# A two-layer hybrid decoder on one core: norm sums of the first layer from a token-major copy of x, early MLP items of four row tiles, and another issue order of the odd norm

## The chip, the cores and the metric

The kernel runs on one core of one Trainium2 chip. The metric is device time in microseconds of one execution, the median of three runs. Five engines work beside each other, each through its own in-order queue: PE (TensorE, matrix products), DVE (VectorE), ACT (ScalarE), POOL (GpSimd) and SP (SyncE, which here issues all DMAs of weights and inputs).

## What is computed

The reference is a decoder trunk of two layers over 1024 tokens of 1024 features in float32. Cut to what matters here:

```
def rmsnorm(x, g):
    y = x * lax.rsqrt(jnp.mean(x * x, axis=-1, keepdims=True) + NORM_EPS)
    return y * g

for layer in range(2):
    hn = rmsnorm(h, mix_norm[layer])
    if layer % 2 == 0:
        h = h + sparse_pool_mixer(hn, ...)   # indexer, top 256 keys a query, attention; causal pooling; one output projection
    else:
        h = h + gated_deltanet(hn, ...)      # projection, short convolution, chunked delta rule
    h = h + squared_relu_mlp(rmsnorm(h, mlp_norm[layer]), w_ff1[layer], w_ff2[layer])
return rmsnorm(h, final_norm)

squared_relu_mlp = lambda h, w1, w2: jnp.square(jax.nn.relu(h @ w1)) @ w2     # 1024 -> 4096 -> 1024
```

## The kernel before

**Layout and products.** The tokens are worked in two halves of 512. Features lie on partitions, so x is eight tiles of 128 x 512 a half, and a norm's sum over features goes over partitions. Every product of float32 operands is made of three matmuls (`mm3`, L244 to L246): high by high, high by low and low by high part. A weight chunk of 128 x 512 comes by DMA from SP (L199), ScalarE copies its high part (L164), GpSimd takes the rest (L168, `rest`); a buffer ring holds four raw chunks. SP issues the loads in the order of the program, with eight semaphores in turn.

**Norms.** `add_square` squares a tile on ScalarE (L304) and adds it to a sum on VectorE (L307). `rstd_cols` sums over partitions with small matmuls against ones (L287), and `rsqrt` makes the reciprocal root on VectorE (L263 to L268). `over_partitions` (L275) spreads it by four transposes, and `normed` scales the tiles. The first half of the even norm is written out in `even_first` (squares, adds at L416), beside the first two projections, which take x with its gain but not yet its scale; `even_second` does the second half through `squares`.

**The even layer.** First projections, scores of the indexer, and the search for the top 256 keys of each query on VectorE and ScalarE (L630 to L698; the last part, L694 to L698, picks the keys of one block of queries). Attention of the second half (`attend`, L710 to L774) comes after the search. Beside the later search and the attention a generator `fill` puts out the MLP of the first half in items: `f1` products (`project`), their squared ReLU (`squared`, L809 to L811 and L168), and `f2` products, which `accumulate` adds into the residual h (L825). In `mlp_order` an item group is two row tiles of the hidden 4096, so each of eight tiles of h gets six matmuls and one VectorE add a group. `even_out` is the output projection of a half, from the attention's tiles and the pool mixer's tiles `yb`; for the second half it runs when `fill` has reached a set point. What is left of the first half's MLP runs in `alone`.

**The odd layer.** `odd_heads` begins with the odd norm of the first half beside the second half's MLP: `norm_stages` gives out squares, then the root, then the normed tiles, each at a `next(norm)`, between items of `fill`:

```
for n in (3, 2, 2):
    for _ in range(n):
        next(fill)
    next(norm, None)
```

A list scheduler orders each engine's instructions from this program order, priorities (`high_priority`, `ahead_by`) and `queued()`, which ties a step to the last matmul issued.

Of the kernel before, what the change touches and what calls it, by code (L numbers as in the profile page):

```python
# [18 lines left out]
OP = mybir.AluOpType  # L19
# [15 lines left out]
FILL = (5.6, 4.7)  # L35
BANKS = {"even": {"g": 2, "o": 1, "s": 1, "t": 4}, "odd": {"g": 2, "o": 1, "d": 2, "t": 3}}
# [87 lines left out]
class Trunk:  # L124
# [257 lines left out]
    def even_scales(self, acc):  # L382

        r = self.rstd_cols(acc, D, self.small(4, "even_r"))
        n8 = self.small(4, "even_n8")
        self.nc.vector.tensor_scalar(n8, r, -0.125, None, op0=OP.mult)
        r8 = self.small(4, "even_r8")
        self.nc.vector.tensor_scalar(r8, r, 0.125, None, op0=OP.mult)
        self.scales.append((r, n8, r8))

    def even_first(self):
# [9 lines left out]
        acc = self.T.get()  # L401
        for k in range(KT):
# [22 lines left out]
        self.even_scales(acc)  # L425
# [389 lines left out]
    def accumulate(self, key, st, a, s, chunks=range(4)):  # L815

        nc = self.nc
        for c in chunks:
            w = [t.rearrange("p (n c) -> p n c", n=2) for t in self.chunk((key, c), st)]
            for m in (2 * c, 2 * c + 1):  # L820
                ps, cs = self.bank("t" if self.solo and m % 2 else "d"), slice(m % 2 * P, (m % 2 + 1) * P)
                for n in range(2):
                    self.mm3(ps, w[0][:, n, cs], w[1][:, n, cs], a[n][:, 0:512], a[n][:, 512:1024], n == 0, n == 1)
                h = self.h[s][m]
                nc.vector.tensor_tensor(h, ps, h, op=OP.add)  # L825
                yield T_ROWS

    def mlp_order(self):

        for g in range(FF // 256 + 1):  # L830
            for n in range(2):
                yield (g if g < FF // 256 else None), n, g - 1, (2 * n, 2 * n + 1)

    def mlp_half(self, l, s, x, ring):

        a = {}
        for g, n, before, chunks in self.mlp_order():  # L840
            if g is not None:
                ps = self.project(("f1", l, 2 * g + n), x, st="m")
                if n == 0:
                    a[g] = [self.squared(ps, ring)]
                self.pending = n == 1
                yield T_COLS
            if before >= 0:
                yield from self.accumulate(("f2", l, before), "m", a[before], s, chunks)
            if g is not None and n == 1:
                a[g].append(self.squared(ps, ring))  # L850
                self.pending = False

    def mlp_units(self, l):
        out = []
        for g, n, before, chunks in self.mlp_order():
            if g is not None:
                out += [((("f1", l, 2 * g + n), c), self.I["w1"][l, 2 * g + n][:, c * 512:(c + 1) * 512], 512)
                        for c in range(2)]
            if before >= 0:
                out += [((("f2", l, before), c), self.I["w2"][l, before, c], 512) for c in chunks]  # L860
# [245 lines left out]
    def odd_heads(self, fills):  # L1106
# [107 lines left out]
    def even(self):  # L1214
# [3 lines left out]
        with ExitStack() as st:  # L1218
# [12 lines left out]
            with ExitStack() as st3:  # L1231
# [9 lines left out]
                for n, _ in enumerate(self.even_steps(0, x, EVEN_A, first)):  # L1241
                    if n == 7:
# [41 lines left out]
            fill = self.mlp_half(0, 0, self.x0, self.Y)  # L1284
            take(fill, 12)
            while self.background:
                take(fill, 2)
                self.tick(1)
            st2.close()
            with ExitStack() as st2:  # L1290
# [3 lines left out]
                for _ in range(8):  # L1294
# [11 lines left out]
        return fill  # L1306
# [58 lines left out]
    def run(self):  # L1365
        a, b = self.odd_units()
        m = [self.mlp_units(l) for l in range(2)]
        self.plan(a=self.even_units() + a, o=b, m=m[0] + m[0] + m[1] + m[1])
        self.h = [[None] * KT, [None] * KT]
        with ExitStack() as st:  # L1370
            self.banks("even", st)
            fill = self.even()
# [3 lines left out]
        self.alone(fill, "below", 3 * len(m[0]))  # L1376
        below = lambda: self.mlp_half(0, 1, x, self.Y)

        def above():
# [3 lines left out]
            yield from self.mlp_half(1, 0, xa, self.Y)  # L1383
# [8 lines left out]
        self.alone(self.mlp_half(1, 1, x, self.Y), "above", 0)  # L1392
# [3 lines left out]
def layouts(x, mix_norm, mlp_norm, w_ff1, w_ff2, ev_w_in, ev_kv_norm, ev_w_uk, ev_w_uv, ev_pool_w, ev_pool_scale,  # L1396
# [11 lines left out]
    def pairs(w):  # L1408

        return c(w.reshape(-1, 2, P, 4, 256).transpose(0, 3, 2, 1, 4).reshape(-1, 4, P, 512))  # L1410

    cols = lambda v: np.asarray(v).reshape(-1, P).T
# [7 lines left out]
        "xt": c(x[0].T), **const_tables(), "prm": c(prm), "rope": rope_table(),  # L1420
# [4 lines left out]
        "woo": pairs(od_w_out[0]), "w1": np.stack([tiles(w) for w in w_ff1]), "w2": np.stack([pairs(w) for w in w_ff2]),  # L1425
    }
# [21 lines left out]
```

## Time and profile before

| | us |
|---|---|
| three runs | 2812.59, 2803.46, 2809.56 |
| median | 2809.56 |
| profiled execution, its own time | 2807.27 |
| its span, first to last instruction | 2805.5 |
| TensorE busy | 2652.1 (95%) |
| VectorE busy | 1702.2 (61%) |
| GpSimd busy | 1229.8 (44%) |
| ScalarE busy | 1185.3 (42%) |

The profile is of one execution, in us from its first instruction. TensorE's matmuls are pipelined: a row's duration is longer than the distance to the next. The granted clock is the share of TensorE's full speed that the chip let it have. "Idle before" an instruction is put down to what released it last.

### The profile page before, as it was taken

Reading aid. Unit: us, or ns where it says so; the run is one execution under the profiler, and the core shown is the slowest. Engines: PE = TensorE matmul, PEld = TensorE weight load, DVE = VectorE, ACT = ScalarE, POOL = GpSimd, SP = SyncE. Lnnn points to the kernel's source line nnn. Section 1 sums busy time; section 2 is a strip of 40 time slices with the busy share of each in tenths; the row PEclk is TensorE's granted clock in tenths of the full one; section 3 lists DMA queues with packets and bytes.
Section 4 is the critical chain, followed back from the end, with each engine's and each line's share of the span. In section 5 each row is a group of like instructions: output and inputs, shape, how many; then the busy total and the mean of one; then the engine's idle time right before and its main releaser. Section 6 shows DMA issues by size and latency. Waiting matters only on the chain. (4 is left out here: it accounts for less than half of the span.)

```text
span 2805.5 us, 44654 instructions
## 1 busy us (share of the span) xinstructions
PE 2652.1 (95%) x16648; PEld 2093.2 (75%) x16648; DVE 1702.2 (61%) x3649; ACT 1185.3 (42%) x2472; POOL 1229.8 (44%) x1062
## 2 busy tenths in 40 slices
PE   8788979999999899999999999999999999899998
PEld 6566758787787677777777767777777777688886
DVE  6898899735535555655565677665555645633334
ACT  5657767234533443433333444433343323433332
POOL 5642364442235444444444434444443434544442
PEclk9999989999999999999999999999999999999999
DMA  5221233231123222222222211122222222333332
GB/s 174 65 75 31 66 97 96 85 94 57 39 65 97 68 80 72 83 69 72 74 77 76 72 43 61 60 70 71 70 83 76 65 65 87 120 97 96 98 97 77
DMA packets 119916, 218.81 MB, mean 78 GB/s; under 512 B 13970, under 2 KB 15122, under 8 KB 119698
## 3 DMA queue, kind: packets, MB, share of 16 engines
q1 hardware_dynamic: 119698, 215.95, 25.1%
q8 instruction: 131, 2.15, 0.3%
q14 instruction: 87, 0.71, 0.1%
HBM read 207.51 MB, written 4.19 MB: 75 GB/s over the span
## 5 line engine op out<-in xcount | busy, mean ns | idle before, releaser
L168 POOL TENSOR_TENSOR wm<-raw,wm 128x512 fp32r<-128x512 f32 x420 | 555.4, 1323 | 843.4 <-ACT wm L164 825.2
L164 ACT ACTIVATE wm<-raw 128x512 fp32r<-128x512 f32 x420 | 264.1, 629 | 612.1 <-PE ps_g L245 306.5
L168 POOL TENSOR_TENSOR w<-raw,w 128x512 fp32r<-128x512 f32 x222 | 297.1, 1339 | 374.3 <-ACT w L164 348.5
L825 DVE TENSOR_TENSOR h<-ps_d,h 128x512 f32<-128x512 f32 x396 | 269.9, 685 | 139.3 <-PE ps_d L246 136.6
L811 DVE SCALAR_TENSOR_TENSOR ps_g<-ps_g,temps 128x512 f32<-128x512 f32 x128 | 89.2, 696 | 308.0 <-ACT temps L809 308.0
L244 PE MATMUL ps_g<-x,w 128*128 128x512 f32 (+1 forms) x644 | 257.6, 400 | 12.0 <-ACT w L164 8.9
L245 PE MATMUL ps_g<-x,w 128*128 128x512 f32 x644 | 256.0, 398 | 3.3 <-DVE x L379 2.5
L244 PE MATMUL ps_d<-y,wm 128*128 128x512 f32 x600 | 246.8, 412 | 11.8 <-DVE h L825 8.0
L246 PE MATMUL ps_g<-x,w 128*128 128x512 f32 (+1 forms) x644 | 255.5, 397 | 1.0 <-POOL w L168 1.0
L164 ACT ACTIVATE w<-raw 128x512 fp32r<-128x512 f32 x222 | 139.0, 627 | 275.5 <-PE ps_g L245 190.1
L245 PE MATMUL ps_d<-y,wm 128*128 128x512 f32 x600 | 238.8, 398 | 0.0
L246 PE MATMUL ps_d<-y,wm 128*128 128x512 f32 x600 | 238.4, 397 | 0.1
L246 PE MATMUL ps_g<-xb,wm 128*128 128x512 f32 x512 | 205.0, 400 | 15.6 <-POOL wm L168 15.6
L244 PE MATMUL ps_g<-xb,wm 128*128 128x512 f32 x512 | 205.6, 401 | 3.9 <-ACT qkvz L930 2.3
L932 DVE SCALAR_TENSOR_TENSOR qkvz<-temps,conv,qkvz 128x512 f32<-128x512 f32 x144 | 133.9, 930 | 122.3 <-ACT qkvz L930 121.1
L245 PE MATMUL ps_g<-xb,wm 128*128 128x512 f32 x512 | 204.3, 399 | 0.0
L244 PEld LDWEIGHTS ps_g<-x,w 128*128 128x128 f32 (+1 forms) x644 | 122.0, 190 | 41.1 <-ACT w L164 9.6
L244 PE MATMUL ps_g<-x,wm 128*128 128x512 f32 x348 | 141.3, 406 | 9.3 <-ACT wm L164 5.2
L246 PE MATMUL ps_g<-x,wm 128*128 128x512 f32 x348 | 140.3, 403 | 10.0 <-POOL wm L168 10.0
L825 DVE TENSOR_TENSOR h<-ps_t,h 128x512 f32<-128x512 f32 x180 | 123.2, 687 | 43.6 <-PE ps_t L246 43.3
L245 PEld LDWEIGHTS ps_g<-x,w 128*128 128x128 f32 x644 | 121.6, 189 | 32.9 <-DVE x L379 4.6
L244 PEld LDWEIGHTS ps_d<-y,wm 128*128 128x128 f32 x600 | 112.7, 188 | 44.0 <-DVE h L825 14.2
(430 smaller groups left out, 6159.1 us busy)
## 6 DMA issues: line engine op xcount, KB each, us to landing
raw<-in_w_dram SPq DMA_DIRECT2D x512, 256.0 KB, 2.6
raw<-in_woi_dram SPq DMA_DIRECT2D x128, 256.0 KB, 2.6
raw<-in_wei_dram SPq DMA_DIRECT2D x52, 256.0 KB, 2.7
raw<-in_weo_dram SPq DMA_DIRECT2D x32, 256.0 KB, 2.6
raw<-in_woo_dram SPq DMA_DIRECT2D x32, 256.0 KB, 2.7
h<-in_xt_dram SPq DMA_DIRECT2D x16, 256.0 KB, 3.5
at<-at SPq DMA_DIRECT2D x64, 64.0 KB, 2.0
out_dram<-temps SPq DMA_DIRECT2D x16, 256.0 KB, 2.1
```

Source lines behind the costliest of these rows:

```text
L164: self.nc.scalar.activation(out, in_, AF.Copy)
L168: eng.tensor_tensor(lo, full, hi.bitcast(F32), op=OP.subtract)
L244: mm(ps, wh, xh, start=start, stop=False)
L245: mm(ps, wh, xl, start=False, stop=False)
L246: mm(ps, wl, xh, start=False, stop=stop)
L811: nc.vector.scalar_tensor_tensor(ps, ps, 0.0, r, op0=OP.max, op1=OP.mult)
L825: nc.vector.tensor_tensor(h, ps, h, op=OP.add)
L932: nc.vector.scalar_tensor_tensor(acc, pin[:, j:j + 512], cw(j), acc, op0=OP.mult, op1=OP.add)
```

## The change

**Sums of the even norm.** A second copy of x, `xr`, with tokens on partitions, comes in as 16 more loads of 128 x 512 (256 KB each). `even_sums` squares each in place on ScalarE and sums along the row in the same instruction (`accum_out`); `even_scales` adds the two half sums and takes the root. The adds at L416, the small matmuls for these two norms and the squares and adds of `even_second` are gone. The second half's sums are issued beside the first projections.

**Items of four.** 28 of the 32 row tiles of the first half's MLP (`EARLY` = 7 groups) go in groups of four, with a second arrangement of the `f2` weights (`w2q`): a tile of h gets twelve matmuls in one PSUM bank and one add a group, so 56 adds fewer in all. The squared tiles take the rings `Y` and `PB` in turn. The items are paced by their estimated time (`beside`), all 28 tiles are issued ahead of `even_out` of the second half, and the splits of its `yb` tiles (a ScalarE copy and a GpSimd rest each, four tiles) go to the attention's own ring `pb`, so they can only come when attention is done with it. Before, they were at 349.98 to 358 us. The last four row tiles stay in groups of two, in `alone`.

**The odd norm.** The first `next(norm)` comes ahead of the first items.

```diff
+    def even_sums(self, s, cs):
+        nc = self.nc
+        for c in cs:
+            for n in range(2):
+                t = self.H[1].get()
+                at = s * HL + c * P
+                nc.sync.dma_start(t, self.I["xr"][at:at + P, n * 512:(n + 1) * 512])
+                nc.scalar.activation(t, t, AF.Square, accum_out=self.sums[s][:, 4 * n + c:4 * n + c + 1])
-    def even_scales(self, acc):
-        r = self.rstd_cols(acc, D, self.small(4, "even_r"))
+    def even_scales(self, s):
+        t, m = self.sums[s], self.small(4, "rs_m")
+        self.nc.vector.tensor_tensor(m, t[:, 0:4], t[:, 4:8], op=OP.add)
+        self.nc.vector.tensor_scalar(m, m, 1.0 / D, EPS, op0=OP.mult, op1=OP.add)
+        r = self.rsqrt(m, 4, self.small(4, "even_r"))
...
             self.gained(h, k, x)
-            sq = self.T.get() if k else acc
-            nc.scalar.activation(sq, h[k], AF.Square)
-            if k:
-                nc.vector.tensor_tensor(acc, acc, sq, op=OP.add)
+            if k >= 4:
+                self.even_sums(0, (k - 4,))
...
-        self.even_scales(self.squares(hs))
...
-            for m in (2 * c, 2 * c + 1):
-                ps, cs = self.bank("t" if self.solo and m % 2 else "d"), slice(m % 2 * P, (m % 2 + 1) * P)
-                for n in range(2):
-                    self.mm3(ps, w[0][:, n, cs], w[1][:, n, cs], a[n][:, 0:512], a[n][:, 512:1024], n == 0, n == 1)
-                h = self.h[s][m]
+            for m in range(4 // n):
+                ps, cs = self.bank("t" if self.solo and m else "d"), slice(m * P, (m + 1) * P)
+                for k in range(n):
+                    self.mm3(ps, w[0][:, k, cs], w[1][:, k, cs], a[k][:, 0:512], a[k][:, 512:1024], k == 0, k == n - 1)
+                h = self.h[s][4 // n * c + m]
                 nc.vector.tensor_tensor(h, ps, h, op=OP.add)
...
-        for n in (3, 2, 2):
+        for n in (4, 2, 2):
+            next(norm, None)
             for _ in range(n):
                 next(fill)
-            next(norm, None)
...
                 for n, _ in enumerate(self.even_steps(0, x, EVEN_A, first)):
+                    if n < 2:
+                        self.even_sums(1, (2 * n, 2 * n + 1))
+                    if n == 2:
+                        self.even_scales(1)
...
-            fill = self.mlp_half(0, 0, self.x0, self.Y)
-            take(fill, 12)
+            fill, due = self.mlp_half(0, 0, self.x0, (self.Y, self.PB), 0, EARLY, 4), 0.0
+            def beside(us):
+                nonlocal due
+                due += us
+                while due > 0:
+                    if len(self.queue["m"]) < self.after_early + 8:
+                        self.room("m", self.WM)
+                    due -= next(fill, 1e9)
+            beside(27.0)
             while self.background:
-                take(fill, 2)
+                beside(4.5)
                 self.tick(1)
...
-                    take(fill, 2)
+                    beside(4.5)
                 for _ in att:
-                    take(fill, 1)
-            self.room("m", self.WM)
-            while self.pending or any(t[3] is not self.WM for t in self.ready["m"]):
-                next(fill)
-            for _ in self.even_out(1, ya, self.yb[1], self.PB):
-                pass
+                    beside(3.0)
+                beside(1e6)
+                for _ in self.even_out(1, ya, self.yb[1], pb):
+                    pass
```

How the order of instructions moves, at three places. Lines of the changed kernel are shifted: L288 is the old L287, L276 the old L275, L308 the old L307, L836 the old L825, L822 the old L811, L169 the old L168, L704 to L709 the old L693 to L698, and L244 to L246 are now L245 to L247.

PE at the odd norm of the first half (`ps_d`: the last `f2` products of the fill; L287: sums over partitions; L275: the root spread; `x,w`: odd projections of the first half; `xb`: fill of the second half), before:

```order
3058 L245 MATMUL ps_d<-y,wm 128x512
3059 L246 MATMUL ps_d<-y,wm 128x512
3060 L287 MATMUL ps_t<-ca,temps 128x2 x4
3061 L275 MATMUL ps_t<-ca,rs_y 128x128 x4
3062 L244 MATMUL ps_g<-x,w 128x512
3063 L244 MATMUL ps_g<-xb,wm 128x512
```

and now, with 16 more rows of the same `ps_d` products where the dots are:

```order
3043 L247 MATMUL ps_d<-y,wm 128x512
3044 L288 MATMUL ps_t<-ca,temps 128x2 x4
3045 L245 MATMUL ps_d<-y,wm 128x512
...
3062 L247 MATMUL ps_d<-y,wm 128x512
3063 L276 MATMUL ps_t<-ca,rs_y 128x128 x4
3064 L245 MATMUL ps_g<-xb,wm 128x512
3065 L246 MATMUL ps_g<-xb,wm 128x512
```

The sums and the spreading, neighbours before, now have 18 full matmuls between them; ahead of L288 stand 72 `xb` and 6 `ps_d` matmuls, and behind L276 24 `xb` matmuls before the first `x,w`.

DVE at the same place, before (L825: residual adds, of the second half here; L307: adds of squares of the first half):

```order
1269 L825 TENSOR_TENSOR h_7283<-ps_d,h_7283 128x512
1270 L168 TENSOR_TENSOR y<-ps_g,y 128x512
1271 L307 TENSOR_TENSOR temps<-temps 128x512
1272 L825 TENSOR_TENSOR h_7323<-ps_d,h_7323 128x512
1273 L307 TENSOR_TENSOR temps<-temps 128x512
1274 L825 TENSOR_TENSOR h_7363<-ps_d,h_7363 128x512
1275 L307 TENSOR_TENSOR temps<-temps 128x512
1276 L825 TENSOR_TENSOR h_7403<-ps_d,h_7403 128x512
1277 L307 TENSOR_TENSOR temps<-temps 128x512 x4
1278 L289 TENSOR_SCALAR rs_m<-ps_t 128x4
```

and now (h_101 to h_104 are tiles of the first half):

```order
1194 L836 TENSOR_TENSOR h_101<-ps_d,h_101 128x512
1195 L308 TENSOR_TENSOR temps<-temps 128x512
1196 L836 TENSOR_TENSOR h_102<-ps_t,h_102 128x512
1197 L308 TENSOR_TENSOR temps<-temps 128x512
1198 L836 TENSOR_TENSOR h_103<-ps_d,h_103 128x512
1199 L308 TENSOR_TENSOR temps<-temps 128x512
1200 L836 TENSOR_TENSOR h_104<-ps_t,h_104 128x512
1201 L308 TENSOR_TENSOR temps<-temps 128x512 x2
1202 L822 SCALAR_TENSOR_TENSOR ps_g<-ps_g,temps 128x512
```

The adds of squares follow the first half's own last residual adds, and the second half's items come behind them.

DVE at the search's end (the selection of the last two blocks, score_88 and score_89), before:

```order
876 L694 TENSOR_SCALAR junk<-score_88,ps_s 128x896
877 L695 SCALAR_TENSOR_TENSOR junk<-junk 128x896
878 L697 TENSOR_SCALAR score_88<-score_88,ps_s 128x896
879 L696 SCALAR_TENSOR_TENSOR junk<-junk,tk_t_3850 128x896
880 L698 SCALAR_TENSOR_TENSOR mask_80<-junk,score_88 128x896
881 L630 TENSOR_SCALAR junk,tk_cnt<-score_89,ps_s 128x1024
882 L693 TENSOR_SCALAR tk_t_3850<-tk_cnt 128x1
883 L694 TENSOR_SCALAR junk<-score_89,ps_s 128x1024
884 L811 SCALAR_TENSOR_TENSOR ps_g<-ps_g,temps 128x512
885 L825 TENSOR_TENSOR h_97<-ps_t,h_97 128x512
```

and now:

```order
843 L705 TENSOR_SCALAR junk<-score_88,ps_s 128x896
844 L706 SCALAR_TENSOR_TENSOR junk<-junk 128x896
845 L708 TENSOR_SCALAR score_88<-score_88,ps_s 128x896
846 L707 SCALAR_TENSOR_TENSOR junk<-junk,tk_t_3784 128x896
847 L709 SCALAR_TENSOR_TENSOR mask_80<-junk,score_88 128x896
848 L641 TENSOR_SCALAR junk,tk_cnt<-score_89,ps_s 128x1024
849 L822 SCALAR_TENSOR_TENSOR ps_g<-ps_g,temps 128x512
850 L704 TENSOR_SCALAR tk_t_3784<-tk_cnt 128x1
851 L705 TENSOR_SCALAR junk<-score_89,ps_s 128x1024
852 L169 TENSOR_TENSOR y<-ps_g,y 128x512
853 L836 TENSOR_TENSOR h_101<-ps_t,h_101 128x512
```

The run of the selection is as long as before; fewer adds are due behind it.

SP at the start, before (`xt`: x with features on partitions, `wei`: projection weights, `at`: an on-chip copy):

```order
13 L397 DMA h_104<-in_xt_dram 128x512
14 L410 DMA ca<-in_ca_dram 128x130
15 L411 DMA ce<-in_ce_dram 128x456
16 L199 DMA raw<-in_wei_dram 128x512 x4
17 L1240 DMA wkv<-in_wkv_dram 128x320
18 L449 DMA rope<-in_rope_dram 128x1024
19 L199 DMA raw<-in_wei_dram 128x512 x3
20 L436 DMA probs<-in_xt_dram 128x2x512
```

and now:

```order
19 L425 DMA ce<-in_ce_dram 128x456
20 L390 DMA h_212<-in_xr_dram 128x512
21 L390 DMA h_215<-in_xr_dram 128x512
22 L390 DMA h_227<-in_xr_dram 128x512
23 L390 DMA h_230<-in_xr_dram 128x512
24 L200 DMA raw<-in_wei_dram 128x512 x4
25 L1252 DMA wkv<-in_wkv_dram 128x320
26 L200 DMA raw<-in_wei_dram 128x512 x2
27 L390 DMA h_331<-in_xr_dram 128x512
28 L390 DMA h_334<-in_xr_dram 128x512
```

Four of the first half's new loads stand ahead of the third projection's weights (four more among the last tiles of `xt`), and all eight of the second half's come ahead of the position table `rope` or right behind it.

## Rows read from the trace of the kernel before

**Rows 1.** The page: TensorE's share of the span (busy us, share, instructions of each engine) and the granted clock in 40 equal slices.

```profile
PE 2652.1 (95%) x16648; PEld 2093.2 (75%) x16648; DVE 1702.2 (61%) x3649; ACT 1185.3 (42%) x2472; POOL 1229.8 (44%) x1062
PEclk9999989999999999999999999999999999999999
```

**Rows 2.** The table of stretches in steps of 50 us: length, then busy us and instructions of PE, its weight loads, DVE, ACT and POOL, the granted clock, the DMA share and GB/s.

```profile
0.00:50.00 50.00, 39.20 (x173) 28.47 (x174) 32.33 (x57) 24.04 (x42) 23.13 (x21) 1.00 0.62 201
50.00:100.00 50.00, 42.43 (x179) 34.10 (x179) 37.86 (x78) 27.07 (x51) 36.28 (x30) 0.93 0.24 73
...
450.00:500.00 50.00, 50.00 (x222) 41.19 (x221) 47.63 (x104) 30.02 (x53) 25.22 (x19) 1.00 0.32 100
500.00:550.00 50.00, 44.46 (x183) 35.58 (x182) 39.60 (x48) 13.94 (x23) 21.69 (x16) 0.93 0.26 79
...
900.00:950.00 50.00, 40.78 (x164) 31.66 (x164) 27.53 (x45) 22.16 (x39) 26.64 (x21) 0.86 0.24 74
```

**Rows 3.** The same table for short stretches with a lower clock, with the same columns.

```profile
919.00:931.00 12.00, 3.29 (x14) 2.49 (x12) 8.14 (x20) 1.68 (x4) 3.19 (x2) 0.61 0.16 44
931.00:936.00 5.00, 4.70 (x12) 3.50 (x13) 5.00 (x8) 2.77 (x5) 4.40 (x3) 0.56 0.01 2
...
517.00:526.00 9.00, 5.22 (x13) 4.15 (x14) 8.93 (x13) 1.51 (x4) 1.27 (x1) 0.62 0.18 60
...
374.00:394.00 20.00, 8.19 (x17) 3.97 (x16) 19.72 (x20) 9.95 (x18) 17.62 (x11) 0.63 0.24 67
82.00:100.00 18.00, 15.80 (x73) 12.82 (x72) 18.00 (x51) 10.04 (x19) 9.87 (x8) 1.00 0.17 56
```

**Rows 4.** PE's instructions in order of time at the odd norm: start, duration, instruction, and in brackets the idle time before it and what ended it.

```profile
924.39 1.86 PE L287 MATMUL ps_t<-ca,temps 128*128 128x2 f32 x8 [5.07 <-DVE temps L307]
928.68 1.11 PE L275 MATMUL ps_t<-ca,rs_y 128*128 128x128 f32 x4 [2.43 <-DVE rs_y L268]
931.30 0.79 PE L244 MATMUL ps_g<-x,w 128*128 128x512 f32 x1 [1.50 <-ACT x L164]
```

**Rows 5.** DVE in order of time before the odd norm.

```profile
897.05 0.69 DVE L825 TENSOR_TENSOR h<-ps_t,h 128x512 f32<-128x512 f32 x1 [0.68 <-PE ps_t L246]
...
916.30 0.68 DVE L307 TENSOR_TENSOR temps<-temps 128x512 f32<-128x512 f32 x1
...
919.96 4.37 DVE L307 TENSOR_TENSOR temps<-temps 128x512 f32<-128x512 f32 x4
```

**Rows 6.** ACT in order of time there.

```profile
896.87 0.63 ACT L164 ACTIVATE wm<-raw 128x512 fp32r<-128x512 f32 x1 [2.11 <-PE ps_t L245]
...
914.37 0.62 ACT L304 ACTIVATE temps<-h 128x512 f32<-128x512 f32 x1
```

**Rows 7.** PE in order of time at the search's end.

```profile
516.42 0.39 PE L246 MATMUL ps_g<-x,wme 128*128 128x512 f32 x1
520.78 0.77 PE L244 MATMUL ps_t<-y,wm 128*128 128x512 f32 x1 [3.97 <-DVE h L825]
```

**Rows 8.** DVE in order of time there: the scan of one selection, and the first residual add behind it.

```profile
509.54 2.99 DVE L695 TENSOR_TENSOR_SCAN junk<-junk 128x896 uint16<-128x896 bf16 x1
...
519.95 0.68 DVE L825 TENSOR_TENSOR h<-ps_t,h 128x512 f32<-128x512 f32 x1
```

**Rows 9.** DVE's groups of instructions from 410 to 550 us: count, busy us, mean ns, idle time before.

```profile
L825 DVE TENSOR_TENSOR h<-ps_t,h 128x512 f32<-128x512 f32 x47 | 31.6, 681 | 2.0 <-PE ps_t L246 2.0
```

**Rows 10.** The instructions of line L416: durations in ns (least, median, most), and when the first and last start.

```profile
L416 DVE TENSOR_TENSOR temps<-temps x7: 677/682/1782, 8.8 to 19.6; 128x512 f32<-128x512 f32 x7
```

**Rows 11.** PE in order of time at the end of the first projections.

```profile
22.53 0.95 PE L287 MATMUL ps_t<-ca,temps 128*128 128x2 f32 x8
```

**Rows 12.** The accumulator reads on ACT that follow a summing instruction in the search (L657, 80 to 260 us).

```profile
L657 ACT ACTIVATION_READ_ACCUMULATOR junk<-h,tk_cand x31: 185/187/198, 96.6 to 188.9; 128x1 f32 x31
```

**Rows 13.** The DMA view of 0 to 50 us: GB/s in 40 slices, and the whole.

```profile
GB/s 0 86 272 247 213 251 351 403 398 382 396 330 368 298 33 0 184 136 120 224 265 362 339 344 334 261 208 80 92 0 206 305 125 0 0 157 157 105 0 0
DMA packets 5794, 10.04 MB, mean 201 GB/s; under 512 B 672, under 2 KB 1440, under 8 KB 5792
```

**Rows 14.** PE's waits from 0 to 60 us: in total, times, longest.

```profile
PE ps_g L244 <- ACT w L164: 8.9, 2, 6.5
```

**Rows 15.** The instructions of line L307 from 60 to 130 us, and PE's wait for it (us, times).

```profile
L307 DVE TENSOR_TENSOR temps<-temps x7: 675/1175/1792, 83.2 to 91.9; 128x512 f32<-128x512 f32 x7
...
  PE ps_t L287: 2.2, 1
```

**Rows 16.** DVE and POOL in order of time at 83 to 87 us.

```profile
83.24 0.68 DVE L307 TENSOR_TENSOR temps<-temps 128x512 f32<-128x512 f32 x1
85.30 1.79 DVE L307 TENSOR_TENSOR temps<-temps 128x512 f32<-128x512 f32 x1
...
84.74 1.80 POOL L168 TENSOR_TENSOR wm<-raw,wm 128x512 fp32r<-128x512 f32 x1 [4.32 <-ACT wm L164]
```

**Rows 17.** The last attention tile, all engines in order of time: the sum, the copy, the split.

```profile
795.69 0.69 DVE L774 TENSOR_TENSOR temps<-ps_o,temps 128x512 f32<-128x512 f32 x1 [1.57 <-PE ps_o L740]
...
796.42 0.63 ACT L164 ACTIVATE q<-temps 128x512 fp32r<-128x512 f32 x1 [1.45 <-DVE temps L774]
...
797.13 1.29 POOL L168 TENSOR_TENSOR q<-temps,q 128x512 fp32r<-128x512 f32 x1 [17.66 <-ACT q L164]
```

**Rows 18.** PE's waits from 370 to 412 us: in total, times, longest.

```profile
PE ps_g L246 <- POOL wm L168: 4.7, 2, 3.9
```

More of the change, by code (lines that the diff above doesn't have):

```diff
@@ L400, in even_first @@
         pss = [self.bank("g") for _ in keys]
-        acc = self.T.get()
+        self.sums = [self.small(8, "even_sums") for _ in range(2)]
         for k in range(KT):
@@ L828, in mlp_order @@
[L828 to L840, printed above, removed]
+            w = [t.rearrange("p (n c) -> p n c", n=n) for t in self.chunk((key, c), st)]
+            for m in range(4 // n):
[3 more added lines that the diff above has]
+                h = self.h[s][4 // n * c + m]
+                nc.vector.tensor_tensor(h, ps, h, op=OP.add)
+                yield T_ROWS * n / 2
@@ L841, in mlp_half, with mlp_order @@
+    def mlp_order(self, first, last, size):
+        for g in range(first, last + 1):
+            for n in range(size):
+                yield (g if g < last else None), n, (g - 1 if g > first else None), (2 * n, 2 * n + 1)
+    def mlp_half(self, l, s, x, rings, first=0, last=FF // 256, size=2):
+        a, count = {}, 0
+        for g, n, before, chunks in self.mlp_order(first, last, size):
             if g is not None:
-                ps = self.project(("f1", l, 2 * g + n), x, st="m")
-                if n == 0:
-                    a[g] = [self.squared(ps, ring)]
@@ L845, in mlp_half @@
-                self.pending = n == 1
+                ps = self.project(("f1", l, size * g + n), x, st="m")
+                ring, count = rings[count % len(rings)], count + 1
+                if n < size - 1:
+                    a.setdefault(g, []).append(self.squared(ps, ring))
                 yield T_COLS
-            if before >= 0:
-                yield from self.accumulate(("f2", l, before), "m", a[before], s, chunks)
-            if g is not None and n == 1:
+            if before is not None:
+                yield from self.accumulate(("f2", size, l, before), "m", a[before], s, chunks)
@@ L850, in mlp_half, with mlp_units @@
+            if g is not None and n == size - 1:
                 a[g].append(self.squared(ps, ring))
-                self.pending = False
-    def mlp_units(self, l):
+    def mlp_units(self, l, first=0, last=FF // 256, size=2):
         out = []
-        for g, n, before, chunks in self.mlp_order():
+        for g, n, before, chunks in self.mlp_order(first, last, size):
             if g is not None:
-                out += [((("f1", l, 2 * g + n), c), self.I["w1"][l, 2 * g + n][:, c * 512:(c + 1) * 512], 512)
+                out += [((("f1", l, size * g + n), c), self.I["w1"][l, size * g + n][:, c * 512:(c + 1) * 512], 512)
@@ L858, in mlp_units @@
                         for c in range(2)]
-            if before >= 0:
-                out += [((("f2", l, before), c), self.I["w2"][l, before, c], 512) for c in chunks]
+            if before is not None:
+                w2 = self.I["w2"][l] if size == 2 else self.I["w2q"]
+                out += [((("f2", size, l, before), c), w2[before, c], 512) for c in chunks]
         return out
@@ L1371, in run @@
             self.banks("even", st)
-            fill = self.even()
+            self.even()
         self.banks("odd", self.stack)
@@ L1375, in run @@
         x = self.normed(self.h[1], R_MLP, self.norm_scale(self.h[1]), XB)
[L1376 to L1377 removed]
+        self.alone(self.mlp_half(0, 0, self.x0, [self.Y], 2 * EARLY), "below", 3 * len(m[0]))
+        below = lambda: self.mlp_half(0, 1, x, [self.Y])
         def above():
@@ L1391, in run @@
         self.finish(0)
-        self.alone(self.mlp_half(1, 1, x, self.Y), "above", 0)
+        self.alone(self.mlp_half(1, 1, x, [self.Y]), "above", 0)
         self.finish(1)
```

19 lines of the change are left out of this document (11 added, 8 removed).

## The prediction, before the changed kernel ran

> **What bounds the kernel now.** I read the engine shares of the page first: TensorE is busy for 2652.1 of 2805.5 us, 95%, at a granted clock that is at its upper level (2.4 GHz) in nearly all slices [rows 1]. So the change can only win time where TensorE is idle or at a lower clock. The table of stretches shows where: from 450 to 500 us TensorE has no gap (50.00 of 50.00 us, 222 matmuls, so 0.225 us for one), though VectorE is busy too; but 0 to 50, 50 to 100, 500 to 550 and 900 to 950 us have 39.20, 42.43, 44.46 and 40.78 [rows 2]. The last two stretches hold one stall each, and a tail at half clock behind it: 0.62 around the first, 0.61 and 0.56 around the second, where 1.00 is the upper level and 0.50 the lower one [rows 3]. The single instructions around these gaps [rows 4 to 8] say what ended each. In 0 to 300 us the search on VectorE sets much of the pace, beside projections on TensorE.
>
> **The odd norm (squares given out first).** At 924.39 TensorE waits 5.07 us for the last add of squares (L307), then 2.43 us for the reciprocal root, then 1.50 us for the first normed tile: 9.0 us in a row, because the small matmuls L287 and L275 follow each other with nothing between [rows 4]. The last residual add was done at 897.05, but the adds of squares only begin at 916.30 and end at 924.3 [rows 5]; ScalarE gave the first square at 914.37, though it idled 2.11 us at 896.87 [rows 6]. The cause is issue order alone. What the stall costs with its clock: 900 to 950 us has 164 matmuls, 12 of them small ones of the norm; 152 x 0.225 = 34.2 us, plus some 1.5 for the small ones, so 14.3 of 50 us are lost. The change issues squares and adds among the last residual adds; its TensorE order has 72 + 6 full matmuls (17.6 us) from the fill ahead of L287, 18 (4.1 us, over the 2.43 of the root) between L287 and L275, and 24 (5.4 us, over the 1.50) before the first that needs a normed tile. All three waits are covered. I take **11.5 us** and leave 3 for a shorter wait elsewhere; bounds 7 (the first wait alone with its clock: 14.3 x 5.07 / 9.0 = 8.1, less 1 for the fill that is now spent earlier) and 14.3. If the cover fails, the root's 2.43 us is the next wait.
>
> **The search's end (items of four tiles).** At 520.78 TensorE waits 3.97 us for a residual add (L825) [rows 7]. VectorE was in the last selection: from the scan at 509.54 to the add at 519.95 it ran search instructions and one squaring step, no residual add, for 10.4 us [rows 8]. TensorE fills its four "t" banks in the meantime: six matmuls each, 4 x 6 x 0.225 = 5.4 us. With items of four tiles each bank takes twelve, so the same banks last 10.8 us, about as long as that run. The loss before: 183 matmuls against 222 in 500 to 550, 39 x 0.225 = 8.8 us. In the changed order the four instructions of a selection still stand in a row, but the adds between them are half as many. I take **6.5 us**; bounds 2 (only half of the 3.97 goes: the squaring step still waits in the same queue) and 8.8. The rest of the saved adds, 56 in all at 681 ns = 38 us of VectorE [rows 9], I cost at nothing: TensorE has no gap in 450 to 500 [rows 2], and it is the cover. The matmuls are the same in number, and the early weight loads too (109 before, 112 now).
>
> **The even norm, first half.** Gone are seven adds (L416), 677 to 1782 ns, 6.5 us of VectorE between 8.8 and 19.6 us [rows 10], eight squares on ScalarE, and eight small matmuls of 0.95 us [rows 11]. New are eight loads of 256 KB ahead of the third projection's weights on SP's queue, and eight squares on ScalarE that wait for them, each with an accumulator read like those of 187 ns in the search [rows 12]: 1.5 us more ScalarE. Another eight loads follow for the second half; behind them on SP's queue stand the position table and the second half's x. In all 4.19 MB. The queue moved 380 to 400 GB/s at best and 201 on average in these 50 us [rows 13], so 10.6 us at 395 or 20.9 at 201. TensorE already waits 8.9 us there for a split of the weights [rows 14]. What goes from VectorE and what comes to the queue are of a size: I take **0**, bounds -9 (that wait doubles, since ScalarE's squares stand in order in front of the splits) and +3 (half of the 6.5 us).
>
> **The even norm, second half.** Seven adds (L307), 675 to 1792 ns and 7.7 us together, stand on VectorE between 83.2 and 91.9 us among the scores and the search, and TensorE waits 2.2 us for them [rows 15]. They go; the new sums are ready long before. In 82 to 100 us VectorE has no idle time [rows 3], so up to 7.7 + 2.2 = 9.9 us come back. Two of these adds took 0.68 and 1.79 us; the slow one ran beside a split on POOL that took 1.80 [rows 16], where a split alone takes 1.29 [rows 17]. Undisturbed, the seven are 7 x 0.68 = 4.8 us, the lower bound: whatever VectorE runs beside those splits next may be slowed in turn. I take **6 us**, between the two. The Trainium skill (GPSIMD Engine Reference, 1. Specifications) says that GpSimd shares its SBUF interfaces with VectorE and contends with VectorE instructions that read two SBUF inputs. By that rule only the 4.8 us would come back and the total would be 2787 instead of 2786; these rows agree with it.
>
> **The stretch 374 to 410 us.** The even layer's output of the second half and the start of the fill: clock 0.63 and 8.19 of 20 us in 374 to 394 [rows 3], waits on POOL's weight splits of 4.7 us [rows 18]. The change takes four splits of the pool mixer (4 x 1.29 on POOL) from about 350 to 358 us, but not the wait: **0**, bounds -2 and +3.
>
> **The attention's end.** These four splits now stand on POOL right ahead of the last attention tile's split, and no MLP item is left to cover it. Before, VectorE's sum at 795.69, ScalarE's copy at 796.42 and POOL's split at 797.13 to 798.42 [rows 17] ran under 18 matmuls of the fill. The bare chain is 2.7 us. If the four splits also come late: 4 x 1.29 = 5.2 more, less what POOL does earlier, where it had idled 17.66 us. I take **-2.5**, bounds -7 and 0.
>
> **The sum:** 0 + 6 + 0 + 6.5 - 2.5 + 11.5 = 21.5 us off the profiled 2807.3 us (span 2805.5) gives **2786 us**. The three runs have a median of 2809.6, 0.08% above, which I leave out.
>
> **Rivals.** *Gains eaten:* the odd norm gives 11.5, the rest nothing, and the attention's end costs 7: 4.5 us, 2803 us. For it: the selection's instructions still stand in a row in the new order, and the start is loaded with transfers; against: the second half's adds are plainly on a full VectorE. *More:* the second half gives 9.9, the search's end 8.8, the odd norm 14 with the attention's end at nothing: 32.7 us, 2775 us. For it: VectorE's relief early also moves the search's end forward. *Slower, by the start:* the 16 loads stand in SP's in-order queue ahead of weights, and ScalarE's squares, in order too, stand ahead of the weight splits. If the projections wait for the whole 20.9 us, and each us of waiting costs what it did at the odd norm (14.3 for 9.0), 33 us go against 21.5: 2819 us. It decides from a start stall of 13.5 us on (13.5 x 14.3 / 9.0 = 21.5), and from 18.8 us on it is slower by more than 0.3%. Against: TensorE has other work there, and the loads come in two parts. *The change does not do what it says:* the items of four could fill no better, since TensorE is the bound there; that is within the first rival.
>
> **Numbers.** 0.3% is 8.4 us, about what a measurement of this kernel tells from no change. Forecast 0.65, more 0.15 (both faster: 0.80), eaten 0.13 (same), start stall 0.07 (slower). The range is 2770 to 2803: it takes in the case of more with a little beyond it, and the eaten case's better half; the start stall and the other half are left out. The bounds of the terms added up reach from a gain of 39 us to a loss of 4, all at once, which I hold unlikely.
>
> **What would show it.** Right: no wait over 1 us at L287 and L275 of the odd norm and the clock at 1.00 there; a shorter wait than 3.97 us at the last selection; at the scores of the second half no VectorE adds of squares; at the attention's end a gap of 2 to 4 us before the output projection. Wrong: TensorE idle for more than 10 us between 20 and 60 us with weights or ScalarE named; a gap of over 7 us at the attention's end; or a wait of the same size at the selection, since then the number of adds was not its cause.

## The result, and the profile after

The changed kernel takes 2783.6 us (median; 2779.9 to 2785.0) against 2806.5 us beside it: a ratio of 0.9916, 95% interval 0.989 to 0.9943. Timed again later (a2_full), it had 0.9926 (0.9913 to 0.9938). The forecast was 2786 us. So the sum came out; its terms did not all, as the places below show. One of the eleven executions of e3_xr took 5492.3 us, a slow one, and no ratio below counts it. Lines of the changed kernel are shifted as in the section on the change.

The page of the profile after, TensorE's share and the granted clock:

```profile
PE 2646.7 (95%) x16632; PEld 2090.6 (75%) x16632; DVE 1658.8 (60%) x3581; ACT 1188.3 (43%) x2488; POOL 1227.9 (44%) x1062
PEclk9999989999999999999999999999999999999999
```

The table of stretches of the kernel after, with the columns of [rows 2]:

```profile
0.00:50.00 50.00, 39.11 (x156) 28.62 (x157) 28.74 (x59) 27.80 (x60) 17.49 (x18) 0.93 0.70 238
50.00:100.00 50.00, 41.04 (x164) 32.82 (x163) 35.21 (x65) 23.55 (x43) 36.46 (x32) 0.90 0.35 111
...
450.00:500.00 50.00, 50.00 (x220) 40.95 (x219) 47.35 (x91) 24.85 (x44) 28.35 (x19) 1.00 0.30 95
500.00:550.00 50.00, 49.44 (x216) 40.13 (x215) 26.51 (x32) 16.99 (x28) 24.49 (x19) 1.00 0.32 97
...
900.00:950.00 50.00, 46.91 (x204) 34.98 (x203) 30.30 (x45) 21.32 (x36) 26.65 (x24) 0.97 0.27 85
```

Against [rows 2]: the search's end (500 to 550) has 216 matmuls for 183, the odd norm (900 to 950) 204 for 164. The start has won nothing: 156 and 164 for 173 and 179, and the clock there is lower. By 300 us the two kernels are about level again (1139 matmuls for 1148).

**The odd norm.** TensorE in order of time, as [rows 4]:

```profile
912.41 0.95 PE L288 MATMUL ps_t<-ca,temps 128*128 128x2 f32 x8
...
920.94 0.65 PE L276 MATMUL ps_t<-ca,rs_y 128*128 128x128 f32 x4 [2.97 <-DVE rs_y L269]
```

The first wait (5.07 us) and the third (1.50) are gone, the second is 2.97 us, although 18 matmuls stand between, and the clock is lower around it:

```profile
914.00:926.00 12.00, 8.91 (x33) 6.65 (x32) 11.23 (x22) 4.00 (x7) 6.65 (x5) 0.86 0.27 88
```

The root that took 2.43 us now takes 7.5 (913.39 to 920.88). Some of its steps, on VectorE between residual adds:

```profile
915.50 1.22 DVE L267 SCALAR_TENSOR_TENSOR rs_t<-rs_y 128x4 f32<-128x4 f32 x1
916.75 1.22 DVE L268 TENSOR_TENSOR rs_t<-rs_t,rs_m 128x4 f32<-128x4 f32 x1
918.00 0.16 DVE L269 SCALAR_TENSOR_TENSOR rs_y<-rs_t,rs_y 128x4 f32<-128x4 f32 x1
```

and GpSimd at the same time:

```profile
915.41 1.29 POOL L169 TENSOR_TENSOR wm<-raw,wm 128x512 fp32r<-128x512 f32 x1 [2.37 <-ACT wm L165]
916.66 1.29 POOL L169 TENSOR_TENSOR w<-raw,w 128x512 fp32r<-128x512 f32 x1
```

A step on four elements a partition, 0.16 us by itself, takes 1.22 us beside a split: it ends at 916.72 us, 0.02 us behind the split that began before it, and the next one ends at 917.97, 0.02 behind the next split. Three steps of this root met a split, for some 3.2 us more; a step of the MLP and three residual adds that stand between its steps add about 2.4.

**The search's end.** The wait of 3.97 us is gone; the longest of TensorE's waits from 500 to 530 us is now

```profile
PE ps_t L246 <- DVE probs L169: 0.6, 1, 0.6
```

and VectorE's residual adds from 410 to 550 us are 23 for the 47 of [rows 9]:

```profile
L836 DVE TENSOR_TENSOR h<-ps_t,h 128x512 f32<-128x512 f32 x23 | 15.7, 684 | 5.3 <-PE ps_t L247 5.3
```

**The even norm.** TensorE's waits from 40 to 110 us (total, times, longest), before:

```profile
PE ps_t L370 <- POOL y L358: 4.3, 2, 4.0
PE ps_t L287 <- DVE temps L307: 2.2, 1, 2.2
PE ps_t L370 <- POOL y L359: 1.4, 2, 1.1
```

and after:

```profile
PE ps_t L371 <- POOL y L359: 7.6, 2, 4.0
PE ps_t L371 <- POOL y L360: 1.4, 2, 0.7
```

VectorE has idle time in 82 to 100 us now (busy for 13.16 of 18 us), and the wait for the adds of squares is gone. But the scores' first matmuls wait 3.3 us more for the query stacks (POOL y). Some 20 us earlier TensorE runs at its lower clock for a while. Before and after:

```profile
30.50:37.50 7.00, 6.45 (x33) 4.52 (x35) 3.84 (x16) 1.42 (x3) 1.69 (x2) 1.00 0.48 151
```

```profile
30.50:37.50 7.00, 6.66 (x20) 5.60 (x21) 2.84 (x14) 4.49 (x14) 0.00 (x0) 0.53 0.66 218
```

The same work takes 2.9 us longer: the first of these matmuls begins at 30.94 us before and at 30.84 after, those of L477 (now L488) at 36.23 and 38.99. The low clock is in this stretch in five of the seven profiles with token-major sums and in none of the six without; e5_seam, the same up to here, is without it. What lowers it is not shown.

**The attention's end and the seam behind it.** No gap is at the attention's end (793 to 800 us, columns as above):

```profile
793.00:800.00 7.00, 7.00 (x67) 5.94 (x65) 2.28 (x4) 4.75 (x10) 4.49 (x5) 1.00 0.38 118
```

The four splits ran on GpSimd from 792.33 us on, under the last attention matmuls, and the projection worked on their tiles until the split of the last attention tile (799.93) had begun:

```profile
792.33 1.29 POOL L169 TENSOR_TENSOR probs<-h,probs 128x512 fp32r<-128x512 f32 x1 [9.50 <-ACT probs L165]
...
796.08 2.52 POOL L169 TENSOR_TENSOR probs<-h,probs 128x512 fp32r<-128x512 f32 x2 [0.72 <-ACT probs L165]
...
799.93 1.29 POOL L169 TENSOR_TENSOR q<-temps,q 128x512 fp32r<-128x512 f32 x1 [1.33 <-PE ps_g L245]
```

The loss is some 60 us later, where the last four row tiles start a pipeline of their own. From 800 to 900 us before and after:

```profile
800.00:900.00 100.00, 98.23 (x434) 80.08 (x433) 46.19 (x72) 36.26 (x63) 52.82 (x42) 1.00 0.29 91
```

```profile
800.00:900.00 100.00, 95.35 (x410) 76.18 (x409) 48.88 (x71) 39.88 (x69) 53.39 (x42) 0.98 0.28 90
```

24 matmuls fewer in the same time, all of full size, 24 x 0.225 = 5.4 us. Two of the gaps, 2.7 us, are the restart: the first `f2` waits for its squared tile, the next `f1` for the bank of the one before. Another 8 of the 24 are missing in 840 to 850 us, where the clock is 0.83 (1.00 before).

```profile
859.48 0.50 PE L245 MATMUL ps_d<-y,wm 128*128 128x512 f32 x1 [1.41 <-ACT y L821]
...
861.95 0.50 PE L245 MATMUL ps_g<-x,wm 128*128 128x512 f32 x1 [1.26 <-DVE y L169]
```

**A place I had not priced: the odd layer.** TensorE's waits of 950 to 1612 us begin before the change with

```profile
PE ps_g L246 <- POOL wm L168: 10.2, 6, 2.3
```

and after with

```profile
PE ps_g L245 <- ACT qkvz L942: 3.0, 3, 1.0
```

The six waits came at one step of a head. One of them before, on GpSimd and on TensorE:

```profile
1238.74 1.27 POOL L1041 COPY xx<-xxc 32x128 f32<-32x128 f32 x4
1240.05 0.61 POOL L1043 COPY xt<-xtc 32x128 f32<-32x128 f32 x2
1240.74 2.50 POOL L168 TENSOR_TENSOR wm<-raw,wm 128x512 fp32r<-128x512 f32 x2
```

```profile
1242.05 0.50 PE L246 MATMUL ps_g<-xb,wm 128*128 128x512 f32 x1 [2.29 <-POOL wm L168]
```

A weight split of the fill stood behind six copies of the head in GpSimd's queue. My reading is that it does so only if the fill needs a chunk at that step, so that what counts is where the fill stands against the heads: the change issues 4 + 2 + 2 items ahead of the first head, one more than 3 + 2 + 2. The first three experiments test that.

### The profile page after: what moved, and what is told of

Its sections match the earlier page's. It is cut to its first block, busy times and chain, and to the rows that moved or that the text cites. A ratio compares the mean times of both kernels' runs of the same rounds, so it can differ in the third digit from the quotient of the medians.

```text
span 2782.8 us, 44590 instructions
## 1 busy us (share of the span) xinstructions
PE 2646.7 (95%) x16632; PEld 2090.6 (75%) x16632; DVE 1658.8 (60%) x3581; ACT 1188.3 (43%) x2488; POOL 1227.9 (44%) x1062
## 5 line engine op out<-in xcount | busy, mean ns | idle before, releaser
L169 POOL TENSOR_TENSOR wm<-raw,wm 128x512 fp32r<-128x512 f32 x424 | 561.6, 1325 | 850.5 <-ACT wm L165 828.2
L169 POOL TENSOR_TENSOR w<-raw,w 128x512 fp32r<-128x512 f32 x222 | 295.4, 1331 | 351.1 <-ACT w L165 316.7
L836 DVE TENSOR_TENSOR h<-ps_d,h 128x512 f32<-128x512 f32 x392 | 267.2, 686 | 136.3 <-PE ps_d L247 134.7
L245 PE MATMUL ps_g<-x,w 128*128 128x512 f32 x644 | 258.8, 402 | 11.1 <-ACT w L165 8.7
L822 DVE SCALAR_TENSOR_TENSOR ps_g<-ps_g,temps 128x512 f32<-128x512 f32 x128 | 89.2, 697 | 298.5 <-ACT temps L820 298.5
L246 PE MATMUL ps_g<-x,w 128*128 128x512 f32 x644 | 256.2, 398 | 1.9 <-DVE x L380 1.8
L247 PE MATMUL ps_g<-x,w 128*128 128x512 f32 x644 | 255.6, 397 | 1.0 <-POOL w L169 1.0
L245 PE MATMUL ps_d<-y,wm 128*128 128x512 f32 x596 | 243.7, 409 | 11.3 <-DVE h L836 7.6
L247 PE MATMUL ps_d<-y,wm 128*128 128x512 f32 x596 | 236.4, 397 | 0.1
L246 PE MATMUL ps_d<-y,wm 128*128 128x512 f32 x596 | 236.0, 396 | 0.0
L245 PE MATMUL ps_g<-xb,wm 128*128 128x512 f32 x512 | 206.5, 403 | 5.6 <-ACT qkvz L942 5.0
L247 PE MATMUL ps_g<-xb,wm 128*128 128x512 f32 x512 | 205.4, 401 | 5.5 <-POOL wm L169 5.3
L246 PE MATMUL ps_g<-xb,wm 128*128 128x512 f32 x512 | 205.0, 400 | 0.0
L245 PEld LDWEIGHTS ps_g<-x,w 128*128 128x128 f32 x644 | 122.8, 191 | 39.7 <-ACT w L165 9.4
L245 PE MATMUL ps_g<-x,wm 128*128 128x512 f32 x348 | 140.4, 404 | 6.5 <-DVE y L169 2.6
L245 PEld LDWEIGHTS ps_d<-y,wm 128*128 128x128 f32 x596 | 112.0, 188 | 46.1 <-DVE h L836 15.2
L246 PEld LDWEIGHTS ps_g<-x,w 128*128 128x128 f32 x644 | 122.7, 191 | 30.5 <-DVE x L380 4.1
L247 PE MATMUL ps_g<-x,wm 128*128 128x512 f32 x348 | 139.9, 402 | 5.5 <-POOL wm L169 5.5
L247 PEld LDWEIGHTS ps_g<-x,w 128*128 128x128 f32 x644 | 122.4, 190 | 27.6 <-POOL w L169 1.4
```

What stands on the lines that cost most here:

```text
L169: eng.tensor_tensor(lo, full, hi.bitcast(F32), op=OP.subtract)
L245: mm(ps, wh, xh, start=start, stop=False)
L246: mm(ps, wh, xl, start=False, stop=False)
L247: mm(ps, wl, xh, start=False, stop=stop)
L822: nc.vector.scalar_tensor_tensor(ps, ps, 0.0, r, op0=OP.max, op1=OP.mult)
```

## The experiments

Times are ratios to the kernel before, timed beside each; 0.001 is 2.8 us. The kernels e1 to e4 ran on one chip, a2, x1, x2 and e5 on a second, e6 to e8 on a third. Theory 1 was that each part pays at its own place and the odd layer by the one item.

**Order with its one item more (e1_order).**

```diff
-        for n in (3, 2, 2):
+        for n in (4, 2, 2):
+            next(norm, None)
             for _ in range(n):
                 next(fill)
-            next(norm, None)
```

> The kernel before with the third part of the change alone: next(norm) ahead of the items, 4, 2, 2 items. Theory 1 (each part pays at its own place): the odd norm's stall shrinks by some 9 us (one wait of about 3 us left at L275), and the odd layer's waits for GpSimd's weight splits between 1060 and 1600 us go as well, some 10 us more, since the fill stands one item further ahead: 2806 - 19 = 2787 us. Rival (the odd layer's gain comes from the items of four, which end the first half's MLP elsewhere): only the norm's 9 us, 2797 us.

Measured: 0.9942 (0.9928 to 0.9955), -16 us. The odd norm has 203 matmuls in 900 to 950 us, and the six waits for splits are gone. Theory 1's -19 lies inside the interval, the rival's -9 outside.

**One item more, norm not earlier (e2_phase).**

```diff
-        for n in (3, 2, 2):
+        for n in (4, 2, 2):
```

> The kernel before with 4, 2, 2 items in place of 3, 2, 2, and next(norm) behind the items as it was: the fill one item further ahead, the norm not earlier. Theory 1: the norm's stall of 9 us with its clock tail stays, the waits for GpSimd's weight splits between 1060 and 1600 us go: some 2796 us. Rival (these waits go because the norm comes earlier, or because of the items of four): no gain, 2806 us within 3.

Measured: 0.9985 (0.9976 to 0.9994), -4 us; my -10 lies outside the interval. The six waits are gone, so it is not the earlier norm or the items of four that removed them. But others of the same layer grew, the first of them

```profile
PE ps_g L244 <- ACT qkvz L930: 4.2, 5, 1.0
```

and the odd norm still loses most of what it lost (176 matmuls).

**Order without the item (e7_order322).** As e1_order, with 3, 2, 2.

> The kernel before with next(norm) ahead of the items, but 3, 2, 2 items as it had: the order of the norm without the fill one item further ahead. Theory (the odd layer's waits for GpSimd's weight splits depend on how far ahead the fill stands, and on nothing else of the change): the norm's stall shrinks by some 9 us, the six waits of 10.2 us in all between 950 and 1612 us are there as before: a ratio of about 0.996, against 0.994 with 4, 2, 2. Rival (they depend on the norm being early): the waits are gone, a ratio of 0.994 or less.

Measured: 0.9969 (0.9959 to 0.998), -9 us. The norm is better (198 matmuls), and the odd layer's waits are back, as the theory has it:

```profile
PE ps_g L246 <- POOL wm L168: 10.4, 6, 2.3
```

So the order gives 9 us and the one item 8 beside it (16.3 - 8.7), 4 without it.

**Token-major sums alone (e3_xr).** The first part of the change on the kernel before.

```diff
-            sq = self.T.get() if k else acc
-            nc.scalar.activation(sq, h[k], AF.Square)
-            if k:
-                nc.vector.tensor_tensor(acc, acc, sq, op=OP.add)
+            if k >= 4:
+                self.even_sums(0, (k - 4,))
...
+                    if n < 2:
+                        self.even_sums(1, (2 * n, 2 * n + 1))
+                    if n == 2:
+                        self.even_scales(1)
```

> The kernel before with the even norm's sums from the token-major copy alone. Theory 1: no change by 300 us of the program, as in the full change (what VectorE wins at 83 to 92 us comes back as a later first query stack, a wait of 3.5 us at about 52 us): 2806 us within 3. Rival, as I forecast it: the second half's adds and the wait of 2.2 us go, 6 us: 2800 us.

Measured: 1.0006 (0.9997 to 1.0015): no change. Its waits of 40 to 110 us are those of the full change:

```profile
PE ps_t L370 <- POOL y L358: 7.5, 2, 4.0
```

My 6 us are refuted.

**Items of four alone (e4_four).** The full change with the other two parts taken back: the odd norm's loop and the even norm as before. It has the pacing and the new place of the splits too, so it does not test the number of adds by itself.

> The kernel before with items of four tiles and their pacing alone (without the token-major sums, with the old order of the odd norm). Theory 1: the search's end gives some 7 us, 350 to 450 us some 2, the restart of the first half's MLP behind the output projection (at about 850 us) takes 3 to 5: 2801 us within 3, the odd norm's stall and the odd layer's waits as before. Rival (the items of four change where the odd layer starts in the fill): 2790 us or less.

Measured: 1.0007 (0.9998 to 1.0016): nothing, where theory 1 had -5. The profile shows both sides of it:

```profile
500.00:550.00 50.00, 48.03 (x211) 38.97 (x210) 27.16 (x34) 16.33 (x27) 24.41 (x18) 1.00 0.29 91
800.00:900.00 100.00, 96.00 (x403) 76.86 (x402) 41.80 (x64) 35.43 (x62) 51.17 (x41) 0.95 0.28 88
```

28 matmuls more at the search's end (6.3 us), 31 fewer behind the attention (7.0 us).

**The full change again, and with one part left out.** No edit (a2_full); the even norm as before (x1_order_four); the items as before (x2_order_xr).

> The full change once more, beside kernels that leave one part out. Theory 1 (the parts' gains add up, as timed alone: order of the norm -16, token-major sums +2, items of four +2): about 2796 us, and the 2784 us of the first timing were a lucky draw. Theory 2 (two parts help each other): 2784 us within 3 again.

> The change without the token-major sums: order of the odd norm and items of four. Theory 1: -16 + 2, about 2794 us. Theory 2: if the items of four are the part that helps the order, 2784 us within 3: in the order's own place their 7 us at the search's end are no longer lost in the odd norm's and the odd layer's waits.

> The change without the items of four: order of the odd norm and token-major sums. Theory 1: -16 + 2, about 2794 us. Theory 2: the same if the items of four are the part that helps, and 2784 us if it is the token-major sums.

Measured: 0.9926 (0.9913 to 0.9938), 0.9932 (0.992 to 0.9944), 0.9958 (0.9946 to 0.997), each as theory 2 had it with the items of four as the part that helps. Alone, the three parts add up to -16.3 + 1.7 + 2.0 = -12.6 us; the whole has -20.8. The four intervals put together leave some 6 us either way on this difference of 8, so the parts hardly add up.

Which part helps which is not shown. Without the token-major sums 2 us of the whole are missing (within the intervals), without the items of four 9 us. But counted from the order alone (0.9942), the items bring 3 us (x1_order_four) and the token-major sums cost 4.5 (x2_order_xr), both within the intervals. Some 3 us of interplay stand in the profiles at the items' own places (after the change 33 matmuls more at the search's end and 24 fewer behind the attention, 2 us net, where e4_four has -0.7). Against that, the profiles of the full change and of x2_order_xr, 6.6 us apart at their ends (2782.8 and 2789.4), are 5.5 us apart before the first item of the MLP: GpSimd's first split of its input tiles, in the full change and in x2_order_xr:

```profile
372.94 1.71 POOL L169 TENSOR_TENSOR x<-temps,x 128x512 fp32r<-128x512 f32 x1
```

```profile
378.44 1.71 POOL L168 TENSOR_TENSOR x<-temps,x 128x512 fp32r<-128x512 f32 x1
```

This split begins between 369 and 378 us in the seven profiles with token-major sums, between 371 and 376 in the six without. So a start that comes out differently from one profile to the next is a rival to the help between parts, and no run here rules it out.

**The seam covered (e5_seam).** Three `f1` products of the rest ahead of the output projection.

```diff
                 beside(1e6)
+                self.room("m", self.WM)
+                rest = self.mlp_half(0, 0, self.x0, [self.Y], 2 * EARLY)
+                take(rest, 3)
                 for _ in self.even_out(1, ya, self.yb[1], pb):
```

> The full change with three f1 products of the last four row tiles issued ahead of the second half's output projection, in place of behind it. Theory (the full change loses some 5 us at 800 to 900 us because the first half's MLP starts afresh there: the first f2 waits 1.4 us for the squared tile and the next f1 1.3 us, with a clock drop): both waits go, 3 to 5 us less than the full change beside it. Rival (the 5 us come from the output projection's weights or its split tiles): no difference over 2 us.

Measured: 0.9921 (0.9906 to 0.9935) against 0.9926: 1.4 us, not more than the intervals, and less than the theory's 3 to 5. At its place the theory holds; both waits are gone, and 17 of the 24 matmuls are back:

```profile
800.00:900.00 100.00, 97.89 (x427) 78.37 (x426) 48.76 (x74) 42.81 (x74) 53.88 (x43) 1.00 0.30 96
```

**The root later (e6_scales).**

```diff
-                    if n == 2:
-                        self.even_scales(1)
                     if n == 7:
+                        self.even_scales(1)
```

> The full change with the second half's root (even_scales(1), twelve short VectorE instructions) issued at the eighth projection in place of the third. Theory (the token-major sums' gain is lost at the first query stack, which waits at about 52 us behind that root on VectorE and behind the eight squares on ScalarE): the wait of 3.6 us falls to about 1.5, the squares being where they were; in time 2 us at most. Rival (the wait comes from the loads alone, the position table and the weights standing behind x's copy on SP's queue): it stays at 3.6.

Measured: 0.9931 (0.9912 to 0.9949), no difference. The first query stack still waits 3 us, and the root's last step ends the wait now:

```profile
52.49 0.62 PE L371 MATMUL ps_t<-ki,y 128*128 128x384 f32 x2 [3.02 <-DVE even_r L402]
```

My 1.5 us did not come, and the run does not decide between the theories. The root's last step ended at 52.47 us, GpSimd's split of the query stack at 52.43, so the stack was hardly earlier than that. And the scheduler moved little: eleven of the root's steps, two of them slowed to 1.02 and 1.23 us, still stood on VectorE ahead of the additions that make the stack (46.88 us). The trace answers two other questions. VectorE waited for no DMA between 36 and 56 us, here or after the change (39 to 57 us), so the loads did not hold it. And the eight squares were done at 36.2 us here (35.4 after the change), with ScalarE idle for 3.9 us (7.4) behind them, so they did not hold the stack either.

**Three edits at once (e8_all).** e5_seam and e6_scales, and

```diff
-        for n in (4, 2, 2):
+        for n in (4, 3, 1):
```

> The full change with three edits: three f1 products ahead of the second half's output projection, the root of the second half at the eighth projection, and 4, 3, 1 items in place of 4, 2, 2 between the odd norm's stages (six more matmuls between the sums and the spreading). Theory: the wait of 3.0 us at the spreading falls to 1.6 or less, the waits at 858 to 862 us are gone, the first query stack waits 2 us less: 4 to 8 us under the full change, a ratio of about 0.990. Rival (what is won at these places is lost later): 0.9925, as the full change.

Measured: 0.9916 (0.9903 to 0.9929). The seam's waits are gone; the first query stack waits 3.0 us, as in e6_scales; the third edit missed, since the scheduler left 18 matmuls between sums and spreading:

```profile
922.06 0.65 PE L276 MATMUL ps_t<-ca,rs_y 128*128 128x128 f32 x4 [2.96 <-DVE rs_y L269]
```

The ratio is one that the full change has had too, so this version is not shown to be better.

## Why the prediction was right, and where it was not

The time, 2783.6 for 2786, and the direction were right. Of the four signs of being right, two came (the shorter wait at the last selection, no adds of squares at the scores) and two did not: there is a wait of 2.97 us and a clock of 0.86 at the odd norm, and no gap at the attention's end. Step by step:

- **The odd norm:** right in mechanism for the first and the third wait; 11.5 us forecast, some 9 in 900 to 950 us (40 matmuls) and 8.7 timed (e7_order322). "All three waits are covered" was wrong: my cover of 4.1 us over the root's 2.43 failed with a root of 7.5 us, because I took its time from a stretch in which VectorE ran nothing else and GpSimd no split. The 3 us that I left for a shorter wait elsewhere are about the size of this one.
- **The search's end:** right at its place; 6.5 us forecast, 33 matmuls or 7.4 us there. Timed alone, the items of four gave nothing (e4_four), because what they won here was lost behind the attention. That the other saved adds are worth nothing also held: VectorE's busy time fell by 43 us, TensorE's pace in 450 to 500 us stayed.
- **The even norm, second half:** wrong; 6 us forecast, none. The step that failed is "the new sums are ready long before": they are, but their root, on VectorE at 40.72 to 52.70 us, stands ahead of the first query stack. TensorE waits 3.3 us more for that stack, for 2.2 less at the adds. From 45 to 53 us VectorE has no idle time, and five of the root's steps there took 5.5 us, where five undisturbed ones take 0.8. That the root makes the 3.3 us is read from this order; e6_scales, which was to show it, does not. The low clock at 31 to 37 us adds some 3 us. I had priced what left VectorE and not what came to it earlier. The rule that the prediction took from the Trainium skill (GPSIMD Engine Reference, 1. Specifications) would have given 4.8 us; that too is more than the runs show.
- **The first half's start:** taken at 0; no stall by weights came (TensorE's wait for ScalarE's weight copies from 0 to 60 us: 8.7 us, 8.9 before [rows 14]). The rival of the start did not happen.
- **The attention's end:** the price was too low and the place wrong. -2.5 us at the attention's end forecast, nothing there; -5.4 us behind it. I followed the splits that moved and not the fill that was cut in two: a pipeline that ends must start again. Covering the restart brought 17 of the 24 matmuls back at the place, but no time clear of the intervals (e5_seam).
- **The odd layer:** not in the sum, and worth 4 to 8 us; the six waits that went are 10.2 us. I saw that the loop issues one item more and did not ask which queue it would meet further on.

So some 9 us of gain too many (6 at the even norm, 3 at the odd norm) and 3 us of loss too few were balanced in the main by up to 8 that I had not foreseen. The shares were wrong too: I gave 11.5 us to the order of the odd norm and 10 to the other two parts, but timed alone the order with its item gives 16 and each of the others nothing. How they make 21 to 23 us together stays open. That the total came out so close is in good part luck.

## What to carry to other kernels

When a step moves, price what it meets at its new place in each in-order queue, not only what it leaves. When background work beside a periodic stage is shifted by one item, look for waits that come once a period: they may vanish or appear. When background work is split into two pipelines, the second pays its start again unless something covers it.

## What the runs showed of the hardware

A VectorE step with two inputs on 128 x 4 elements takes 0.16 us, but 1.22 us when a GpSimd split of 1.29 us has just begun; it ends 0.02 us behind the split (rows above). This is no single case: in the trace of the kernel after, 40 steps of one kind (SCALAR_TENSOR_TENSOR, 128 x 4) began while a TENSOR_TENSOR of 128 x 512 on GpSimd had more than 0.06 us left. All 40 ended 0.01 to 0.05 us behind it; they took 0.14 to 1.31 us, by what was left of it. The Trainium skill (SBUF — State Buffer, section SBUF: two separate sides) says that the port pair which the two engines share is "an exclusive lock, not a bandwidth split": a GpSimd instruction or a VectorE instruction with two SBUF inputs, whichever starts first, holds it for the whole instruction. These rows agree, down to the 0.02 us. For a chain of short steps such as a root by iteration this is a factor of over seven on each step that meets a split. At 40 to 53 us of the kernel after it shows as well; the second row stands beside a GpSimd product of 1.30 us that began at 46.52 us:

```profile
44.33 0.16 DVE L268 TENSOR_TENSOR rs_t<-rs_t,rs_m 128x4 f32<-128x4 f32 x1
...
46.61 1.23 DVE L267 SCALAR_TENSOR_TENSOR rs_t<-even_r 128x4 f32<-128x4 f32 x1
```
